# Two more turns between the operands of the head and pooling products and the products, and an embedding unit two products later

## The chip, the cores and the metric

The kernel runs on one core of one Trainium2 chip. The metric is the device time in microseconds (us) of one execution; the median of several runs is compared. Times inside an execution are counted from the start of the profiled span.

## The reference

One decoder layer over 1024 tokens of width 1024, in float32. A normalised input goes through one projection `w_in` to 4608 columns: 512 for a pooling branch, 1024 for a recurrence (RG-LRU), 1024 for its GELU gate and 2048 for two sigmoid gates.

```
pooled_g = (csum - csum shifted by w_g)/count - z_pool_g      4 groups of 128, w = 2, 4, 8, 16
y_pool   = (pooled_g @ pool_w_g) * pool_scale  @ pool_proj
xc       = causal convolution of z_lru, width 4
r, ig    = sigmoid(xc_head @ w_rg + b), sigmoid(xc_head @ w_ig + b)      8 heads of 128
a        = exp(-8 r softplus(-lambda));  b = sqrt(1 - a^2) * ig * xc
y_lru    = scan(a, b) * gelu(z_gelu)  @ lru_proj
h        = x + (gate0 * y_pool + gate1 * y_lru) @ w_out
h        = h + (silu(v @ w_g) * (v @ w_u)) @ w_ffn_out,   v = rms_norm(h)
h        = h + sigmoid(rms_norm(h) @ w_ple_gate) * (p @ w_ple_proj)
out      = rms_norm(h)
```

## The kernel before

**Products.** Channels lie on the 128 partitions, the 1024 tokens along the free axis, in two halves LOW and HIGH of 512. Every float32 product is made of three matmuls on split operands: a factor is cast by ScalarE (`hi`, L115) and the remainder of the cast is taken by VectorE (`lo`, L119). `mm3` (L216) issues hi*hi, hi*lo and lo*hi (L219 to L221); `mm6` (L223, matmuls at L227) does the same for both token halves.

**Units.** TensorE's work is a list of units that `drive()` issues in order. The first projection is done with Strassen's scheme (`strassen`): output tiles go in 18 pairs, each pair needs seven products named by `q` in the order 1, 5, 6, 2, 7, 3, 4, and each product is one unit of 12 matmuls. Pairs go in groups of 3, then six groups of 2, then 3, and a group does its first product for each pair, then the second, and so on: 126 units. Ahead of them stand four units of the per-layer embedding `p @ w_ple_proj` (`ple_unit`, also 12 matmuls each), and four more are set among the first projection's units. Counted from 0 that makes units 0 to 133 up to the end of the first projection. Unit 134 is the first of the pooling branch's projection (`w_pproj`, `mm6`, 24 matmuls each, eight units), and then come the recurrence's projection, `w_out`, the feed-forward layer and the embedding gate.

**The turn of a unit.** In the turn of a unit `drive()` issues, in this order: the inserted units that wait (below), each preceded by the `post` of the unit before it; the `post` of the unit before (it takes results out of PSUM); loads of weights, at most two beyond those that are cast; `second` (`lo`) of weights up to three units ahead and `first` (`hi`) up to four ahead; the unit's `pre`; a slice of background work; the unit's matmuls. Each engine works through its own instructions in the order in which they were issued.

**Background.** Convolution, gates and scan of a head (`chain(c, z)`, eight of them), pooling (`pooling(gi, z)`, four) and the reloads are Python generators in a queue. Only the two at the front are stepped. A turn gives a credit of half a unit's nominal time; a step that yields a number costs that many us; a step that yields `None` means: not again before the next turn. Chains with an odd number first let five turns go by. A head's product is two small units of six matmuls (`half(0)`, `half(1)`), a pooling group's two of three; they are put into `inserted` and go out behind the unit in whose turn they were put in. A chain makes the casts of its weights and LOW tokens in one turn (L688 and L689 are the sigmoids of its product, L706 to L708 tanh, exp and square, L712 and L713 VectorE's steps, L715 the square root, L722 to L726 products and scan), and in the turn that puts in `half(0)` it casts the HIGH tokens.

**The end of the first projection.** When the pooled tiles are spilled and the last group's third product has begun, `begin_mixed` (in the queue behind the last chain that was added before it) lets four reloads follow: each loads one pooled tile (`mx`), and then makes `hi` of both halves (L115) and `lo` of both (L119), over four turns. The first unit of `w_pproj`, unit 134, needs all four, in the order 0 to 3. Its `pre` calls `force`, which steps the two generators at the front until all heads' results `y` are stored and all four `mx` operands are made, before the unit's matmuls are issued:

```
def force(*keys):
    while any(k not in have for k in keys):
        for g in list(background)[:2]:
            step(g)
        while inserted:
            u = inserted.popleft()
            u.emit()
            u.post()
```

```
force(*[("y", c) for c in range(NH)], *[("mx", "op", g) for g in range(NG)])
```

**Shared room.** SBUF tiles of 128x1024 come from one pool of 51 buffers, PSUM has 8 banks, loads go out on SyncE's queue (SP), stores on GpSimd's (POOL).

Of the kernel before, what the change touches and what calls it, by code (L numbers as in the profile page):

```python
# [30 lines left out]
NFIRST = 4  # L31
# [33 lines left out]
def hybrid_block(ctx: ExitStack, tc: tile.TileContext, xT, pT, vec, w_in, w_rgig, w_pool,  # L65
# [10 lines left out]
    def at(name, dt=F32):  # L76
        return ap_.tile([P, T], dt, name=name, tag="a", bufs=NA)

    def ps():
        return pp.tile([P, H], F32, name="ps", tag="ps")  # L80
# [6 lines left out]
    def store(out, x):  # L87
        pool.dma_start(out, x)
# [20 lines left out]
    def col(base, i):  # L109
        return cv[:, base + i:base + i + 1]  # L110
# [3 lines left out]
    def hi(op, x):  # L114
        act.copy(op[:, :x.shape[1]], x)  # L115

    def lo(op, x):
        n = x.shape[1]
        dve.tensor_tensor(op[:, H:H + n], x, op[:, :n].bitcast(F32), ALU.subtract)  # L119
# [95 lines left out]
    def mm3(bank, wop, c, xop, first, last, more=False):  # L215


        a, b = wop[:, c * P:(c + 1) * P], wop[:, H + c * P:H + (c + 1) * P]
        pe.matmul(bank, a, xop[:, :H], start=first, stop=False, skip_group_check=more)  # L219
        pe.matmul(bank, a, xop[:, H:], start=False, stop=False, skip_group_check=more)  # L220
        pe.matmul(bank, b, xop[:, :H], start=False, stop=last, skip_group_check=more)  # L221
# [51 lines left out]
    units = []  # L273
# [377 lines left out]
    def chain(c, z):  # L651
        while "xa" not in have:
            yield None
        if c % 2:
            for _ in range(5):
                yield None
        xc = at("xc")
        act.activation(xc, z, AF.Identity, scale=col(C_CW, 3 * NH + c), bias=col(C_CB, c))
        yield None
        for j in (2, 1, 0):  # L660
            d = 3 - j
            dve.scalar_tensor_tensor(xc[:, d:], z[:, :T - d], col(C_CW, j * NH + c), xc[:, d:],
                                     ALU.mult, ALU.add)
            if j == 2:
                wr = at("wrg")[:, :2 * P]
                nc.sync.dma_start(wr, w_rgig[c])
            yield 1.3
        w = at("wrgo", F32R)
        xo = {0: at("xc0", F32R)}
        hi(w, wr)  # L670
        hi(xo[0], xc[:, LOW])
        yield None
        lo(w, wr)
        lo(xo[0], xc[:, LOW])
        yield 1.1
        r, ig = at("r"), at("ig")

        def half(h):
            banks = []

            def emit():
                banks.extend((ps(), ps()))
                for i in (0, 1):
                    mm3(banks[i], w, i, xo[h], True, True)

            def post():
                s = (LOW, HIGH)[h]
                act.activation(r[:, s], banks[0], AF.Sigmoid, bias=col(C_BR, c))  # L688
                act.activation(ig[:, s], banks[1], AF.Sigmoid, bias=col(C_BI, c))  # L689
                have.add(("rg", c, h))  # L690
            return Unit([], emit, post)

        yield None
        inserted.append(half(0))
        xo[1] = at("xc1", F32R)
        hi(xo[1], xc[:, HIGH])
        yield None
        lo(xo[1], xc[:, HIGH])
        yield 0.7
        yield None  # L700
        inserted.append(half(1))
        while ("rg", c, 1) not in have:
            yield None
        th, q = at("th"), at("q")

        act.activation(th, r, AF.Tanh, scale=psp[:, c:c + 1])  # L706
        act.activation(r, r, AF.Exp, scale=nsp[:, c:c + 1])
        act.activation(q, r, AF.Square)  # L708
        dve.tensor_mul(ig, ig, xc)
        yield 1.2  # L710
        yield None
        dve.scalar_tensor_tensor(th, q, 1.0, th, ALU.add, ALU.mult)  # L712
        dve.tensor_scalar(th, th, 0.0, None, ALU.max)  # L713
        yield 1.9
        act.activation(th, th, AF.Sqrt)  # L715
        pool.memset(th[:, 0:1], 1.0)
        while ("gl", c) not in have:
            yield None
        gl = at("gl")
        nc.sync.dma_start(gl, gl_spill[c])  # L720
        yield None
        dve.tensor_mul(ig, ig, th)  # L722
        yield 1.2
        dve.tensor_tensor_scan(ig, r, ig, 0.0, ALU.mult, ALU.add)
        yield 2.3
        dve.tensor_mul(ig, ig, gl)  # L726
        yield 1.2
        store(y_spill[c], ig)
        have.add(("y", c))
# [4 lines left out]
    def pooling(gi, z):  # L734
        while "xa" not in have:
            yield None
        w = 2 << gi
        cur = z
        for i in range(gi + 1):
            d = 1 << i  # L740
            nxt = at("ws")
            pool.tensor_copy(nxt[:, :d], cur[:, :d])
            dve.tensor_add(nxt[:, d:], cur[:, d:], cur[:, :T - d])
            cur = nxt
            yield 1.3
        wr = at("wrp")[:, :P]
        nc.sync.dma_start(wr, w_pool[:, gi * P:(gi + 1) * P])
        dve.tensor_mul(cur[:, :w], cur[:, :w], icnt[:, :w])
        dve.tensor_sub(cur[:, :w], cur[:, :w], z[:, :w])
        dve.scalar_tensor_tensor(cur[:, w:], cur[:, w:], 1.0 / w, z[:, w:], ALU.mult, ALU.subtract)  # L750
        yield 1.6
        wo = at("wpo", F32R)
        xo = {0: at("pl0", F32R)}
        hi(wo, wr)
        hi(xo[0], cur[:, LOW])
        yield None
        lo(wo, wr)
        lo(xo[0], cur[:, LOW])
        yield 0.9
        mx_ = at("mx")  # L760

        def half(h):
            bank = []

            def emit():
                bank.append(ps())
                mm3(bank[0], wo, 0, xo[h], True, True)

            def post():
                act.activation(mx_[:, (LOW, HIGH)[h]], bank[0], AF.Copy, scale=col(C_PS, gi))  # L770
                if h == 1:
                    store(m_spill[gi], mx_)
                    have.add(("mx", gi))
            return Unit([], emit, post)

        yield None
        inserted.append(half(0))
        xo[1] = at("pl1", F32R)
        hi(xo[1], cur[:, HIGH])
        yield None  # L780
        lo(xo[1], cur[:, HIGH])
        yield 0.7
        yield None
        inserted.append(half(1))
        yield 0.1
# [4 lines left out]
    def then(i):  # L790
        def lru(z):
            background.append(chain(i - ZL, z))
            if i == ZL + NH - 1:
                background.append(begin_mixed())

        def pool_(z):
            background.append(pooling(i, z))

        def gelu(z):
            act.activation(z, z, AF.Gelu_apprx_tanh)  # L800
            store(gl_spill[i - ZG], z)
            have.add(("gl", i - ZG))

        def gate(z):
            act.activation(z, z, AF.Sigmoid, bias=col(C_BG, i - ZS))
            store(g_spill[i - ZS], z)
        return gate if i >= ZS else gelu if i >= ZG else lru if i >= ZL else pool_
# [26 lines left out]

    units[NFIRST].early = early
    for i, u in enumerate(beside):
        units.insert(NFIRST + 1 + 2 * i, u)


    def plain(srcs, nk, xs_of, done, pre=None, side=1, order=None):  # L840
# [434 lines left out]
```

## Time and profile before

| | |
|---|---|
| median of 3 runs | 1410.3 us (1408.74 to 1410.36) |
| profiled execution, its own time | 1409.52 us |
| span of its trace | 1407.8 us |
| TensorE (PE) busy | 1364.6 us, 97% |
| VectorE (DVE) busy | 1032.6 us, 73% |
| ScalarE (ACT) busy | 675.3 us, 48% |
| GpSimd (POOL) busy | 86.5 us, 6% |

The profiled execution's own time is 1.7 us over its span. PE is TensorE's matmuls, PEld its weight loads. A PE record lasts longer (0.39 us) than the distance to the next one, since matmuls are pipelined.

### The profile page before, as it was taken

The page shows a single profiled execution, that of the slowest core. Times are in us where ns is not written, and L with a number is a line of the kernel's source. Part 1 is how long each engine was busy: PE and PEld are TensorE (multiplying, and loading weights), DVE is VectorE, ACT ScalarE, POOL GpSimd, SP SyncE. Part 2 cuts the span into 40 slices and gives each one's busy share as a digit, 9 for nine tenths or more (in the row PEclk, how much of TensorE's full clock was granted, in tenths as well). Part 3 has the DMA queues.
Part 4 walks back from the last instruction along what each step waited for, and adds up shares of the span by engine and source line. Part 5 has one row for each costly group of instructions (what it writes and reads, how often), then busy time and mean ns, then how long its engine had stood idle before and what let it go on. Part 6 is the DMA issues. An engine that isn't in the chain of part 4 may idle for free.

```text
span 1407.8 us, 16468 instructions
## 1 busy us (share of the span) xinstructions
PE 1364.6 (97%) x6006; PEld 1121.5 (80%) x6006; DVE 1032.6 (73%) x1523; ACT 675.3 (48%) x1074; POOL 86.5 (6%) x194
## 2 busy tenths in 40 slices
PE   6999999999999999999999999999999999999986
PEld 4787888888788888888888888888888877887865
DVE  5977788888785544566798888888878767768566
ACT  6558665887867112323554444444454422126331
POOL 0003010010000000000001000010110100000000
PEclk8999999999999999999999999999999999999997
DMA  7122143332549224231134334444577798813203
GB/s 315 75 79 95 61 155 111 115 134 99 200 162 400 89 75 147 105 125 43 60 115 152 132 143 148 150 149 165 194 266 269 295 419 303 326 64 120 72 19 120
DMA packets 64737, 220.55 MB, mean 157 GB/s; under 512 B 7312, under 2 KB 9872, under 8 KB 64656
## 3 DMA queue, kind: packets, MB, share of 16 engines
q1 hardware_dynamic: 45936, 151.80, 30.2%
q0 software_dynamic: 18576, 67.64, 11.9%
q8 instruction: 47, 0.77, 0.2%
q14 instruction: 34, 0.28, 0.1%
q10 hardware_dynamic: 144, 0.06, 0.0%
HBM read 147.65 MB, written 71.83 MB: 156 GB/s over the span
## 4 chain that ended last, share of the span: by engine, by line
PE 85%; DVE 6%; ACT 4%; issue 3%; DMA 1%; POOL 1%; DVEq 0%; SPq 0%; ACTq 0%; POOLq 0%
PE ps L221 22%; PE ps L219 22%; PE ps L220 22%; PE ps L227 17%; DVE w L119 1%; DVE ss L328 1%; DMA lT<-fT 1%; PE ps L367 1%; PE ps L345 1%; DVE pg L1139 0%; ACT pg L1137 0%; DVE h L1140 0%; ACT sq L1145 0%; DVE pg L1136 0%; DMA x<-xT 0%
## 5 line engine op out<-in xcount | busy, mean ns | idle before, releaser
L115 ACT CAST w<-wr 128x512 fp32r<-128x512 f32 (+2 forms) x376 | 221.6, 608 | 339.9 <-DVE wr L194 245.0
L119 DVE TENSOR_TENSOR w<-wr,w 128x512 fp32r<-128x512 f32 (+2 forms) x376 | 249.9, 671 | 44.2 <-ACT w L115 43.4
L221 PE MATMUL ps<-xT,w 128*128 128x512 f32 x640 | 249.5, 390 | 1.5 <-DVE w L119 1.4
L219 PE MATMUL ps<-xT,w 128*128 128x512 f32 x640 | 249.4, 390 | 0.1
L220 PE MATMUL ps<-xT,w 128*128 128x512 f32 x640 | 249.1, 389 | 0.0
L219 PE MATMUL ps<-xB,w 128*128 128x512 f32 x480 | 187.2, 390 | 2.1 <-ACT xB L115 1.2
L220 PE MATMUL ps<-xB,w 128*128 128x512 f32 x480 | 187.4, 391 | 1.9 <-DVE xB L119 1.9
L221 PE MATMUL ps<-xB,w 128*128 128x512 f32 x480 | 187.4, 390 | 0.0
L221 PEld LDWEIGHTS ps<-xT,w 128*128 128x128 f32 x640 | 120.1, 188 | 28.1 <-DVE w L119 3.2
L219 PEld LDWEIGHTS ps<-xT,w 128*128 128x128 f32 x640 | 120.2, 188 | 25.1 <-ACT w L115 0.5
L220 PEld LDWEIGHTS ps<-xT,w 128*128 128x128 f32 x640 | 120.1, 188 | 25.1
L220 PEld LDWEIGHTS ps<-xB,w 128*128 128x128 f32 x480 | 90.3, 188 | 21.8 <-DVE xB L119 3.1
L219 PEld LDWEIGHTS ps<-xB,w 128*128 128x128 f32 x480 | 90.2, 188 | 21.5 <-ACT xB L115 1.6
L221 PEld LDWEIGHTS ps<-xB,w 128*128 128x128 f32 x480 | 90.3, 188 | 19.2 <-DVE w L119 0.6
L227 PE MATMUL ps<-m,w 128*128 128x512 f32 x384 | 87.3, 389 | 0.0
L227 PE MATMUL ps<-y,w 128*128 128x512 f32 x384 | 87.2, 389 | 0.0
L227 PEld LDWEIGHTS ps<-y,w 128*128 128x128 f32 x384 | 72.1, 188 | 15.0
L227 PEld LDWEIGHTS ps<-m,w 128*128 128x128 f32 x384 | 72.0, 188 | 14.9
L1068 DVE TENSOR_TENSOR h<-h,ps 128x512 f32<-128x512 f32 x68 | 46.5, 684 | 42.5 <-PE ps L221 42.4
L194 DVE TENSOR_TENSOR wr<-wr 128x512 f32<-128x512 f32 (+1 forms) x104 | 70.4, 678 | 3.0 <-DMA wr<-w_fout 1.2
L219 PE MATMUL ps<-lT,w 128*128 128x512 f32 x176 | 69.0, 392 | 3.4 <-DMA lT<-fT 2.7
L221 PE MATMUL ps<-lT,w 128*128 128x512 f32 x176 | 68.7, 390 | 0.0
(214 smaller groups left out, 2190.3 us busy)
## 6 DMA issues: line engine op xcount, KB each, us to landing
wr<-w_fin SPq DMA_DIRECT2D x44, 512.0 KB, 5.6
fT<-xT POOLq DMA_DIRECT2D x44, 512.0 KB, 5.0
lT<-fT SPq DMA_DIRECT2D x44, 512.0 KB, 7.9
wr<-w_in SPq DMA_DIRECT2D x36, 512.0 KB, 4.3
fB<-xB POOLq DMA_DIRECT2D x33, 512.0 KB, 5.8
lB<-fB SPq DMA_DIRECT2D x33, 512.0 KB, 6.7
g<-z POOLq DMA_DIRECT2D x16, 512.0 KB, 2.9
g<-g SPq DMA_DIRECT2D x16, 512.0 KB, 6.4
```

Of the source, the lines that this page charges most:

```text
L115: act.copy(op[:, :x.shape[1]], x)
L119: dve.tensor_tensor(op[:, H:H + n], x, op[:, :n].bitcast(F32), ALU.subtract)
L194: f(self.place(out), self.place(a), self.place(b))
L219: pe.matmul(bank, a, xop[:, :H], start=first, stop=False, skip_group_check=more)
L220: pe.matmul(bank, a, xop[:, H:], start=False, stop=False, skip_group_check=more)
L221: pe.matmul(bank, b, xop[:, :H], start=False, stop=last, skip_group_check=more)
L227: pe.matmul(bank, w, xop[:, s], start=f, stop=e)
L328: dve.tensor_add(ss, ss, sq)
L345: pe.matmul(m[:, i:i + 1], self.ss[:, t:t + P], mean, start=True, stop=last is None)
L367: pe.matmul(bank[:, i * P:(i + 1) * P], r[:, b + i:b + i + 1].broadcast_to([P, P]), ident, start=True, stop=True)
L1068: dve.tensor_add(h[t][:, s], h[t][:, s], bank)
```

## The change

`chain` and `pooling` each get two more `yield None`: one before each of the two small products is put in. The operands are made where they were, and each product goes out one unit later than before with respect to them. The four embedding units among the first projection's units stood behind its products 0, 1, 2 and 3; the last of them now stands behind product 5 (behind the second product of all three pairs of the first group, and ahead of their third).

```
@@ chain
         yield None
+        yield None
         inserted.append(half(0))
         xo[1] = at("xc1", F32R)
         hi(xo[1], xc[:, HIGH])
         yield None
         lo(xo[1], xc[:, HIGH])
         yield 0.7
+        yield None
         yield None
         inserted.append(half(1))
@@ pooling
         yield None
+        yield None
         inserted.append(half(0))
         xo[1] = at("pl1", F32R)
         hi(xo[1], cur[:, HIGH])
         yield None
         lo(xo[1], cur[:, HIGH])
         yield 0.7
+        yield None
         yield None
         inserted.append(half(1))
@@
     for i, u in enumerate(beside):
-        units.insert(NFIRST + 1 + 2 * i, u)
+        units.insert(NFIRST + (1, 3, 5, 8)[i] + (i == 3), u)
```

## Rows read from the trace of the kernel before

**Rows 1.** The page, busy time of each engine.

```profile
PE 1364.6 (97%) x6006; PEld 1121.5 (80%) x6006; DVE 1032.6 (73%) x1523; ACT 675.3 (48%) x1074; POOL 86.5 (6%) x194
```

**Rows 2.** Windows of the first projection: busy us of each engine, granted clock, DMA.

```profile
43.00:113.00 70.00, 70.00 (x309) 57.93 (x309) 59.86 (x93) 44.98 (x75) 8.26 (x15) 1.00 0.21 77
113.00:117.00 4.00, 1.95 (x8) 1.08 (x7) 2.97 (x5) 3.71 (x6) 3.36 (x8) 1.00 0.00 0
117.00:360.00 243.00, 242.52 (x1069) 200.12 (x1069) 194.67 (x263) 178.49 (x259) 19.01 (x45) 1.00 0.31 113
360.00:390.00 30.00, 27.50 (x114) 20.49 (x113) 23.49 (x28) 25.42 (x33) 3.14 (x7) 1.00 0.55 210
390.00:429.00 39.00, 39.00 (x174) 32.30 (x173) 28.77 (x42) 28.23 (x42) 1.75 (x4) 1.00 0.59 209
```

**Rows 3.** Waits of PE from 43 to 429 us: total, times, longest.

```profile
PE ps L220 <- DVE xc L119: 1.5, 2, 1.0
PE ps L221 <- DVE w L119: 1.4, 3, 0.7
PE ps L219 <- ACT xc L115: 1.0, 1, 1.0
PE ps L219 <- ACT w L115: 0.9, 1, 0.9
```

**Rows 4.** Timeline of PE at the first head's product: start, duration, instruction, [idle before].

```profile
114.53 0.50 PE L219 MATMUL ps<-xc,wrgo 128*128 128x512 f32 x1 [1.05 <-ACT xc L115]
116.03 0.50 PE L220 MATMUL ps<-xc,wrgo 128*128 128x512 f32 x1 [1.00 <-DVE xc L119]
```

**Rows 5.** Windows: ScalarE from 344 to 381 us.

```profile
344.00:381.00 37.00, 35.17 (x151) 27.55 (x150) 24.72 (x32) 36.27 (x41) 2.55 (x7) 1.00 0.46 171
```

**Rows 6.** Timeline of ScalarE, the late weight cast.

```profile
368.01 1.28 ACT L805 ACT_TABLE_LOAD   x1
369.31 1.15 ACT L805 ACTIVATE z<-z,cv 128x1024 f32<-128x1024 f32 x1
370.36 0.60 ACT L115 CAST w<-wr 128x512 fp32r<-128x512 f32 x1
```

**Rows 7.** Timeline of PE around units 130 and 134.

```profile
409.83 0.39 PE L219 MATMUL ps<-xc,wrgo 128*128 128x512 f32 x1
...
416.63 0.39 PE L219 MATMUL ps<-xc,wrgo 128*128 128x512 f32 x1
...
428.87 6.51 PE L227 MATMUL ps<-mx,w 128*128 128x512 f32 x28
```

**Rows 8.** Timeline of ScalarE, the last chain and the last pooled tile.

```profile
417.55 1.15 ACT L805 ACTIVATE z<-z,cv 128x1024 f32<-128x1024 f32 x1 [0.84 <-DVE z L503]
418.61 0.67 ACT L688 ACTIVATE r<-ps,cv 128x512 f32<-128x512 f32 x1
...
420.26 1.16 ACT L706 ACTIVATE th<-r,sc 128x1024 f32<-128x1024 f32 x1
421.43 1.28 ACT L707 ACT_TABLE_LOAD   x1
422.73 1.15 ACT L707 ACTIVATE r<-r,sc 128x1024 f32<-128x1024 f32 x1
423.91 1.06 ACT L708 ACTIVATE q<-r 128x1024 f32<-128x1024 f32 x1
424.99 1.28 ACT L805 ACT_TABLE_LOAD   x1
...
427.85 1.14 ACT L115 CAST mx<-mx 128x512 fp32r<-128x512 f32 x2
```

**Rows 9.** Timeline of VectorE at the same place.

```profile
425.01 1.23 DVE L712 SCALAR_TENSOR_TENSOR th<-q,th 128x1024 f32<-128x1024 f32 x1 [2.69 <-ACT q L708]
426.27 0.69 DVE L713 TENSOR_SCALAR th<-th 128x1024 f32<-128x1024 f32 x1
...
428.59 1.29 DVE L119 TENSOR_TENSOR mx<-mx 128x512 fp32r<-128x512 f32 x2
```

**Rows 10.** Windows of two places where PE started again after waiting; PEclk is the third number from the right.

```profile
39.00:45.00 6.00, 5.25 (x16) 4.19 (x17) 5.79 (x11) 1.78 (x3) 0.00 (x0) 0.72 0.00 0
1347.00:1356.00 9.00, 8.00 (x23) 6.30 (x24) 6.72 (x11) 3.56 (x7) 0.00 (x0) 0.62 0.00 0
```

**Rows 11.** Timeline of PE, the first matmul of the second of these places.

```profile
1348.00 0.79 PE L221 MATMUL ps<-v,w 128*128 128x512 f32 x1 [3.70 <-DVE w L119]
```

**Rows 12.** Timeline of VectorE, the last remainders of the first group's third operand.

```profile
66.84 1.29 DVE L119 TENSOR_TENSOR xT<-x,xT 128x512 fp32r<-128x512 f32 x2
```

More of the change, by code (lines that the diff above doesn't have):

```diff
@@ L693, in chain @@
         yield None
+        yield None
         inserted.append(half(0))
@@ L699, in chain @@
         yield 0.7
+        yield None
         yield None
@@ L776, in pooling @@
         yield None
+        yield None
         inserted.append(half(0))
@@ L782, in pooling @@
         yield 0.7
+        yield None
         yield None
@@ L836, in hybrid_block @@
     for i, u in enumerate(beside):
-        units.insert(NFIRST + 1 + 2 * i, u)
+        units.insert(NFIRST + (1, 3, 5, 8)[i] + (i == 3), u)
     def plain(srcs, nk, xs_of, done, pre=None, side=1, order=None):
```

## The prediction

> **What bounds the kernel.** The page comes first: TensorE (PE) is busy 97% of the span [rows 1], so only what makes PE wait, or ends a wait of PE, can move the time. All parts of the change lie between 43 and 440 us, so the windows of that stretch come next [rows 2]: PE has no idle time from 43 to 113 us and from 390 to 429, 0.48 us in all from 117 to 360, and two places with idle time, 113 to 117 (4.00 - 1.95 = 2.05 us) and 360 to 390 (2.50 us). One unit is 12 matmuls at 243 us / 1069 = 0.227 us, or 2.72 us; a half of a head's product, six matmuls, is 1.36 us. The waits name the causes [rows 3]: the products of heads wait 2.5 us for casts and remainders of `xc`, and the units at 370 to 386 us wait 2.3 us for casts and remainders of weights. The timeline shows the worst of the first kind [rows 4].
>
> **Part 1: heads and pooling one unit later, at their place.** Waits of 1.05 and 1.00 us stand ahead of the first head's product [rows 4]. The recorded idle time understates it, as a record (0.39 us) outlasts the step to the next (0.227 us): start to start the two gaps and a slow step after them take 2.6 us more than three steps would. The second head's product loses 0.75 us likewise and the third 0.1 us. One unit later (2.72 us) all these operands are ready, and the units that move ahead of the product have had their weights for longer than that. Gain 3.4 us; bounds 2.5 (the recorded waits alone) and 3.4.
>
> **Part 2: ScalarE's crowd at 344 to 381 us.** Here ScalarE is busy 36.27 of 37.00 us [rows 5]. Two chains (5 and 6) run their sigmoid, tanh, exp and square root while gelu and gate tiles come out of the group of units 99 to 112; ten activation tables are loaded, 1.30 us each from start to start, and a weight cast comes behind a gate's sigmoid at 370.36 us, when PE already waits for it [rows 6]. Start to start, units 115 to 119 lose 4.35 us in all (1.46, 1.34, 0.33, 0.59, 0.63).
>
> Where do the chains stand after the change? I stepped through the queue by its rules, turn by turn. For the kernel before, this puts all 24 small products where the trace has them; for example the last chain's, behind units 127 and 129 [rows 7]: from 416.63 us one half (1.36) and four units (10.9) lead to 428.87 us, where unit 134 starts. With the change chains 6 and 5 put in their second halves in turns 114 and 116 (before 106 and 109), so their tanh and exp come after the gelu and gate tiles of turns 110 to 113 instead of among them. Summing ScalarE's work by turn with the spacings of [rows 6, 8], it falls behind PE by about 9 us in turn 117, where it was 13 in turn 113; casts are issued four units ahead (10.9 us), which covers 9 and did not cover 13. What remains is VectorE: a scan stands ahead of one weight's remainder there, about 1 us late. But chain 3 now meets the gelu and gate tiles of turns 82 to 85, at which no chain's exp stood before: the same crowd with one chain, about 0.5 to 1 us late. I take 2.0 us of new waits against the 4.35: gain 2.4 us. Bounds: 4.35 (nothing new waits) and 2 us of loss (both places wait, each for 3).
>
> **Part 3: the end of the first projection.** Each chain now holds one of the two places in the queue for two turns more, and each pooling too. The fourth pooling ends in turn 104 (before 95), chains 6 and 5 in 121 and 125 (before 115 and 118). Only then do the reloads and chain 7 come to the front. Before: reloads start in turns 119, 122, 126 and 129, chain 7's halves go out behind units 127 and 129, and when unit 134 comes only chain 7's last multiply and its store are open. After: the first three reloads start in turns 125, 130 and 133, chain 7's first half goes out behind unit 133, its second isn't put in, and the fourth reload has not begun. So `force` ahead of unit 134 issues all that is left, about twelve rounds of steps: the third tile's `hi` and `lo`, the second half, tanh, exp, square and VectorE's L712 and L713, and only behind those the fourth tile's `hi` (ScalarE) and `lo` (VectorE). Unit 134 needs that tile for the last six of its matmuls' 24.
>
> Let T be the end of unit 133. ScalarE starts about 0.5 us after T, with a copy (0.6) and a gate (1.06 from start to start, 417.55 to 418.61 [rows 8]); the first half's two sigmoids (1.15), a weight cast (0.5) and the third tile's two casts (1.1); the second half's sigmoids (1.15), tanh (1.17), the table load (1.30), exp (1.18) and square (1.07) [rows 8]. That is 10.3, so T + 10.8. VectorE follows with 1.26 and 0.69, then the fourth tile's remainders, 1.29 [rows 9] (its casts run beside the first two): T + 14.1. PE has both halves first (2.72), the first three tiles (4.08) and two matmuls and the bank's turn (0.7), so it wants that remainder at T + 7.5. It waits about 6.6 us. Its DMA is not late: four loads of `mx` stood far ahead of their casts, and ScalarE gets there only at T + 10.8.
>
> A wait this long also costs clock. After PE waited 3.70 us the granted clock was 0.5, that is 1.2 GHz instead of 2.4, for some 6 us [rows 10, 11]: 9 us at a mean of 0.62 are 3.4 us lost, some 0.4 of it while PE still stood. After the several short waits before 40 us the loss was 0.28 x 6 = 1.7 us [rows 10]. PE would stand 4.7 us and then start in pieces. I take 2.5; bounds 1.7 and 3.0.
>
> Sum of part 3: 6.6 + 2.5 = 9.1 us lost. Below, with ScalarE not behind at T, 6.2 + 1.7 = 7.9; above, 7.5 + 3.0, and 1.5 if a buffer for the fourth tile comes free only behind L712: 12. The table load is priced by its row, 1.30 us to the next instruction [rows 8].
> The Trainium skill (ScalarE: Activation LUTs, "What ACT_TABLE_LOAD costs") gives a switch of tables about 1.38 us of drain beside the 1.28 of the load. No drain of that length shows in the row; by the page the one switch in this sequence would cost 1.4 us more and the time be 1415.
>
> Nothing later takes the loss back: after 440 us each stage's PE work waits on PE's own order, all engines shift together, and chain 7's result (some 8 us later) is wanted by the recurrence's projection only 43 us after unit 134 starts.
>
> **Part 4: the last embedding unit.** Two product units come 2.72 us earlier, at a place where PE never waits [rows 2]. The first group's third product, which VectorE feeds to the last moment (its last remainders start at 66.84 us [rows 12], its unit at 67.08), starts when it did, for the same units lie ahead of it. VectorE's order is unchanged, ScalarE's two copies and one store on POOL go out two units later, and POOL's next item comes only at 102 us. Six banks are held by the group and two by the embedding unit, all eight; the next bank is asked for three units on. Zero; if the early weights were short, up to 2.7.
>
> **The sum.** -3.4 - 2.4 + 9.1 = +3.3 us: 1409.5 + 3.3 = 1412.8 for the profiled execution, 1413.6 beside the median, which is 0.8 above it.
>
> **Rivals.**
> *The end is hidden:* the fourth tile is not late, because ScalarE is through with chain 7's activations sooner than summed; then only parts 1 and 2 count, 1410.3 - 5.8 = 1404.5. For it: before, the last `mx` remainders ended at 429.9 us, 3 us ahead of need, and it is one tile in four. Against: its `hi` stands behind a square that cannot run before T + 10, and its price decides: while part 3 costs under 5.8 us the kernel is faster. 0.07.
> *The terms cancel:* the crowd of part 2 goes without a trace (4.35) and part 3 is at its low end: 7.9 - 3.4 - 4.35 = +0.2, 1410.5. With the sizes between that and the forecast's own range, 0.23.
> *The crowds grow:* new waits in both places as long as those of before, 9.1 - 3.4 + 2 = +7.7, 1418. For it: three more chains' phases move, buffers are held longer and loads wait for them. Against: in both places fewer tables are loaded per turn. 0.12.
> *The small products wait as before,* since VectorE and ScalarE order nothing differently: +6.7, 1417. Against: their operands were ready at 116 us, and the first product now comes at 116. 0.03.
>
> **Numbers.** The forecast, 1413.6 with its own range of 1411.5 to 1416, holds 0.55. The bound of 0.2% (2.8 us, about what a measurement of this kernel can tell from no change) lies inside that range, at 1413.1; I put 0.44 of the 0.55 above it, as PE's wait in part 3 is the best founded term and its clock cost can only add. With the third and fourth rival that makes 0.59 for slower; the second rival and the rest of the forecast make 0.34 for no change; the first rival, 0.07, is faster. The range leaves out the first rival and the far end of the third: 1409 to 1418.
>
> **What would show it.** Right: no `xc` wait of PE at 113 to 117 us; no waits for weights of this size at 370 to 386; in the turn of unit 134 a wait of PE of 5 to 7 us for `mx`, named by VectorE's L119 or ScalarE's L115, and PEclk 0.5 behind it. Wrong: unit 134 running 5.4 us without a gap; the wait named by a DMA (then a buffer or the queue decides); waits for weights near 280 us or 390 us of over 2 us; a wait of PE between 56 and 70 us (part 4). The prediction fails if ScalarE has the fourth tile's casts ahead of chain 7's activations, for then nearly all of part 3 is gone.

## The result: slower by 11.3 us

| | before | after |
|---|---|---|
| median of 4 runs each | 1410.33 us | 1421.58 us (1420.24 to 1422.97) |
| ratio, with 95% interval | | 1.0074 (1.0057 to 1.009) |
| profiled execution, its own time | 1409.52 us | 1422.97 us |
| span of its trace | 1407.8 us | 1421.3 us |

The forecast was 1413.6 us with a range of 1409 to 1418. The sign is right; the time lies above the range. The page of the kernel after, busy time of each engine (as [rows 1]):

```profile
PE 1371.1 (96%) x6006; PEld 1126.0 (79%) x6006; DVE 1034.1 (73%) x1523; ACT 673.7 (47%) x1073; POOL 87.2 (6%) x194
```

The work is the same, and PE has a smaller share of a longer span. Windows of the kernel after, from the first head's product to the start of the pooling branch's projection (columns as in [rows 2]):

```profile
113.00:117.00 4.00, 4.00 (x20) 3.29 (x19) 3.27 (x5) 3.71 (x6) 3.34 (x8) 1.00 0.00 0
117.00:280.00 163.00, 163.00 (x721) 134.96 (x720) 126.76 (x172) 114.84 (x168) 13.21 (x31) 1.00 0.31 109
280.00:300.00 20.00, 17.18 (x72) 12.98 (x71) 16.74 (x21) 18.76 (x28) 3.45 (x7) 1.00 0.30 122
300.00:385.00 85.00, 85.00 (x376) 70.38 (x375) 65.12 (x90) 66.23 (x91) 5.40 (x12) 1.00 0.36 128
385.00:412.00 27.00, 23.61 (x96) 18.80 (x95) 21.67 (x27) 15.93 (x25) 1.16 (x3) 0.94 0.55 187
...
429.00:445.00 16.00, 10.34 (x34) 7.05 (x33) 8.70 (x11) 15.88 (x23) 0.92 (x3) 0.84 1.03 420
```

PE's idle time at 113 to 117 us and at 360 to 385 us is gone. In its place PE stands at 280 to 300 us (20.00 - 17.18 = 2.82), at 385 to 412 (3.39) and at 429 to 445 (5.66); in the last two the granted clock falls too. The waits of PE in the same stretch (as [rows 3]; left out are those before 43 us and two of 0.3 us for `xc`):

```profile
PE ps L227 <- ACT mx L115: 4.3, 1, 4.3
PE ps L219 <- DVE z L499: 2.6, 1, 2.6
...
PE ps L221 <- DVE w L119: 1.7, 3, 0.8
...
PE ps L219 <- ACT z L497: 1.1, 1, 1.1
PE ps L227 <- DVE mx L119: 0.8, 1, 0.8
PE ps L219 <- ACT w L115: 0.8, 1, 0.8
```

The 4.3 us for `mx` was forecast. The second row was not: `z` at L499 and L497 are no operands. L497 is ScalarE's copy of product 1 of a pair out of its PSUM bank, L499 VectorE's add of product 2; PE waits there for a bank that has not been read yet.

**Where the time went.** Recorded idle time understates a wait, so the table takes from each trace the distances between the starts of successive matmuls, less the undisturbed step of 0.227 us: waits, plus matmuls at half clock (0.43 us apart). "End" is chain 7's product plus the time from the first `mx` matmul to the first `y` matmul over the 43.52 us that it takes before, less 1.36 us for each half of chain 7 that runs inside it. Columns in us; "sum" is against the kernel before; "time" is the difference of the medians on the same chip.

| kernel | heads 105-210 | 250-300 | 360-412 | end | sum | time |
|---|---|---|---|---|---|---|
| before | 3.5 | 0 | 4.4 | 0 | | |
| after | 0 | 3.9 | 5.5 | 9.5 | +11.0 | +11.3 |
| forecast of after | 0 | 0.5 to 1 | 1 | 9.1 | +3.3 | +3.3 |
| e1_embed | 3.5 | 0 | 4.4 | 0 | 0 | +0.8 |
| e2_heads | 0 | 7.2 | 11.3 | 10.4 | +21.1 | +22.7 |
| e3_pools | 3.4 | 2.0 | 9.5 | 6.8 | +13.7 | +13.3 |
| e4_first | 0 | 1.4 | 5.3 | 0.7 | -0.5 | -0.7 |
| e0_before_end | 3.5 | 0 | 4.4 | 0 | 0 | -0.2 |
| e5_end | 0 | 3.9 | 5.5 | 2.3 | +3.8 | +4.7 |
| e8_before_nogelu | 2.0 | 0 | 3.0 | 0 | -2.9 | -1.1 |
| e7_after_nogelu | 0 | 1.5 | 4.3 | 9.5 | +7.4 | +8.6 |
| e9_scan | 0 | 3.9 | 1.1 | 5.6 | +2.7 | +0.4 |
| e10_conv | 0 | 4.5 | 10.5 | 0 | +7.1 | +6.9 |
| f1_phase3 | 0 | 2.0 | 5.1 | 2.5 | +1.7 | +3.7 |
| e11_kept | 0 | 0 | 4.4 | 0 | -3.5 | -5.3 |
| e12_moved | 0 | 0 | 4.8 | 7.2 | +4.1 | +3.3 |
| f2_phase5 | 0 | 0 | 3.3 | 0 | -4.6 | -2.9 |
| f3_phase5b | 0 | 0 | 1.8 | 1.2 | -4.9 | -3.4 |

For after, the sum agrees with the first `y` matmul, which comes at 483.5 us where it came at 472.4. The profiled execution is 13.45 us longer; of the other 2.4, about 1.6 are a granted clock of 0.94 from 1161 to 1191 us, which the profiled execution of before does not have (1.00 at 1150 to 1180). The difference of the medians, 11.3, is nearer to the sum without it.

The sums lie inside the 95% interval of the time, except for e8, e9 and f1, which miss it by 0.3 to 0.6 us. The table leaves out what lies ahead of 105 us, where the profiled executions differ by 1 us and more though their kernels issue nearly the same. So a difference of under 2 us between two rows is read from the trace and is not shown by the times.

### The profile page after: what moved, and what is told of

Read it like the earlier page. It is cut to its first block, busy times and chain, and to the rows that moved or that the text cites. A ratio compares the mean times of both kernels' runs of the same rounds, so it can differ in the third digit from the quotient of the medians.

```text
span 1421.3 us, 16453 instructions
## 1 busy us (share of the span) xinstructions
PE 1371.1 (96%) x6006; PEld 1126.0 (79%) x6006; DVE 1034.1 (73%) x1523; ACT 673.7 (47%) x1073; POOL 87.2 (6%) x194
## 3 DMA queue, kind: packets, MB, share of 16 engines
q0 software_dynamic: 18576, 67.64, 11.8%
## 4 chain that ended last, share of the span: by engine, by line
PE 78%; DVE 9%; ACT 5%; DMA 4%; issue 3%; POOL 0%; DVEq 0%; SPq 0%; ACTq 0%; POOLq 0%
PE ps L219 20%; PE ps L221 20%; PE ps L220 20%; PE ps L227 17%; DMA lT<-fT 2%; DVE w L119 1%; DVE xc L662 1%; ACT w L115 1%; DMA fB<-xB 1%; DVE ss L328 1%; DMA hr<-h 1%; PE ps L367 1%; PE ps L345 1%; DVE wr L194 1%; DVE pg L1143 1%
```

## The experiments

Each kernel was timed in three rounds against the kernel before on the same chip.

**The change taken apart.** `e1_embed` makes only the third hunk of the change, `e2_heads` only the two lines in `chain`, `e3_pools` only the two in `pooling`, `e4_first` only one extra turn, for one product:

```
@@ e4_first, chain
         yield None
+        if c == 0:
+            yield None
         inserted.append(half(0))
```

> Only the last embedding unit is moved. Theory (three separate causes: new waits at the two crowded places, and the forced work ahead of unit 134): none of them hangs on this unit, so 1410.3 within 1 us, with the waits of before at 113 to 117 and 370 to 386 us. Rival (the moved unit takes the last two PSUM banks, or keeps a buffer, and so starts the later waits): 1413 or more.

> Only the chains of the heads get the two turns. By the queue's rules chain 3's exp falls into turn 82 again (the crowd near 280 us) and the work forced ahead of unit 134 again holds chain 7 and two reloads. Theory: -3.4 for the heads, some 4 near 280 us, 0 to 6 near 390, some 9 at unit 134, less the old 4.35: 1416 to 1421. Rival (the poolings' longer stay is what makes the end late): within 3 us of 1410.

> Only the poolings get the two turns. The waits for xc at 113 to 117 us stay (no gain); chain 3's exp comes in turn 79, before the gelu tiles; when unit 134 comes only the last reload's remainders are open, with chain 7 past its square. Theory: no wait near 280 us, a changed one near 380 us, under 2 us at unit 134: 1408 to 1414. Rival (poolings make the end late): 1417 or more.

> One turn more only ahead of the first head's first product. Theory: its waits go (2.6 us), the end of the projection is as before (one round of forced steps), chains 6 and 5 have exp in turns 107 and 112 and so about the crowd of before: 1407.7, between 1405 and 1410. Rival (any shift of the queue costs what it gains): 1410 or more.

Measured: e1_embed 1411.40, ratio 1.0004 (0.9994 to 1.0013); e2_heads 1433.25, 1.0159 (1.0144 to 1.0174); e3_pools 1423.91, 1.0092 (1.0077 to 1.0107); e4_first 1409.92, 1.000 (0.9991 to 1.001). e2_heads and e3_pools came out far above what was expected (1416 to 1421 and 1408 to 1414), and for e3_pools the rival held: the poolings alone make the end late, by 6.8 us. e4_first stands at the upper edge of its range, as near to its rival.

The embedding unit costs nothing that can be told from zero. The chains' lines alone cost twice what the whole change costs, and the poolings' lines alone more than the whole. So the cost is no sum over the edits: each edit moves the chains against the units, and what counts is where they meet. The timelines of PE from 360 to 412 us show it. First e2_heads, then e3_pools, the two longest waits of each:

```profile
399.26 0.50 PE L219 MATMUL ps<-xB,w 128*128 128x512 f32 x1 [1.66 <-ACT w L115]
...
407.95 0.77 PE L219 MATMUL ps<-xB,w 128*128 128x512 f32 x1 [5.41 <-DVE z L499]
```

```profile
396.75 0.50 PE L221 MATMUL ps<-xB,w 128*128 128x512 f32 x1 [2.21 <-DVE w L119]
...
404.21 0.47 PE L219 MATMUL ps<-xB,w 128*128 128x512 f32 x1 [2.16 <-DVE z L499]
```

In both, the add of L499 ends one of them. Near 280 us the whole 7.2 of e2_heads is one wait for a bank, whose copy L497 is late, with half clock behind it:

```profile
291.64 0.79 PE L219 MATMUL ps<-xT,w 128*128 128x512 f32 x1 [3.81 <-ACT z L497]
```

e4_first shows the same in small: it gains the 3.5 us at the heads, and new waits (1.4 at 250 to 300 us, 0.9 more at 360 to 412, 0.7 at the end) take 3.0 of them back.

**The end.** `e5_end` is after, except that unit 134 finishes only the reloads of `mx`, chain 7 goes on in the background, and from there three generators are stepped instead of two. A reload of `y` now waits until its `y` is stored, which `force` had seen to before (not among the lines below). `e0_before_end` puts the same treatment into before.

```
@@ begin_mixed (the generators are kept in mx_left)
-            background.append(reload(m_spill[gi], mixed, gi, "mx"))
+            mx_left.append(reload(m_spill[gi], mixed, gi, "mx"))
+            background.append(mx_left[-1])
@@ pre_pproj
-            force(*[("y", c) for c in range(NH)], *[("mx", "op", g) for g in range(NG)])
+            for g in mx_left:
+                if g in background:
+                    background.remove(g)
+                    finish(g)
+            width[0] = 3
```

> The changed kernel, but ahead of unit 134 only the four mx reloads are carried to their end; chain 7 goes on in the background among the units of the pooling projection (three generators are stepped per turn there). Theory (unit 134 waits for the fourth tile's casts behind chain 7's activations, 9.5 us with the clock): the forced casts then stand right behind the gate tiles, unit 134 waits 0 to 2 us and the clock stays: 1421.6 - 8 = 1413.5, between 1411.5 and 1416. Rival (the late loads of the tiles, or the buffers, set that wait): 1419 or more.

> The kernel before with the same treatment of the end, as a control. Its unit 134 doesn't wait: 1410.3, within 1.5 us either way, if the chain that goes on later delays nothing.

Measured: e5_end 1415.16, ratio 1.0032 (1.0018 to 1.0045), 6.4 us under after; e0_before_end 1410.22, 1.000 (0.9991 to 1.001). The window and PE's timeline of e5_end at that place:

```profile
429.00:445.00 16.00, 14.50 (x62) 11.23 (x61) 7.18 (x12) 10.19 (x18) 1.06 (x2) 1.00 1.03 420
```

```profile
430.30 2.88 PE L227 MATMUL ps<-mx,w 128*128 128x512 f32 x12
434.59 10.69 PE L227 MATMUL ps<-mx,w 128*128 128x512 f32 x43 [1.41 <-ACT mx L115]
```

With chain 7's activations out of the way one wait of 1.41 us is left (2.3 us in the table), and the clock stays at 1.00 where after has 0.84. The waits at 280 and 390 us are those of after (3.9 and 5.5). So the end and the rest are separate costs, and chain 7's sequence ahead of the fourth tile is the cause of most of the end.

**ScalarE's load.** `e7_after_nogelu` and `e8_before_nogelu` are after and before with the GELU replaced by a copy, so GELU's values and its table loads are left out:

```
-            act.activation(z, z, AF.Gelu_apprx_tanh)
+            act.copy(z, z)
```

> The changed kernel with GELU replaced by a plain copy, which leaves the GELU out, so that ScalarE loads two tables less at each of the crowded places where gelu tiles come out. Theory (near 280 us and 390 us ScalarE's lag holds back the copies out of PSUM and the weight casts): the waits of PE near 280 us (3.9) go altogether, those near 390 us (5.5) fall below 3, the loss at unit 134 stays 9 to 10: 1412 to 1415. Rival (chain lengths and buffers, not ScalarE's lag): 1419 or more.

> The kernel before with GELU replaced by a plain copy (left out), the control: the waits of 4.4 us at 370 to 386 us go or fall below 1.5, those of the heads (3.5) stay: 1406 to 1408.

Measured: e7 1419.01, ratio 1.0059 (1.0044 to 1.0074); e8 1409.30, 0.9992 (0.9983 to 1.0001). Near 280 us the loss falls from 3.9 to 1.5, at 360 to 412 only from 5.5 to 4.3: there the wait for L499 stays at 2.51 us. So GELU with its tables makes most of the loss at the first place and little at the second. Both expectations were missed: e7 was to take 1412 to 1415 and came out at its rival's 1419, and e8 was to take 1406 to 1408, with under 1.5 us left at 370 to 386 us (3.0 are left).

**The bank near 390 us.** In the timeline of after, PE first and then VectorE:

```profile
395.84 0.39 PE L221 MATMUL ps<-xB,w 128*128 128x512 f32 x1
398.83 0.75 PE L219 MATMUL ps<-xB,w 128*128 128x512 f32 x1 [2.60 <-DVE z L499]
399.38 0.63 PE L220 MATMUL ps<-xB,w 128*128 128x512 f32 x1
...
402.32 0.39 PE L221 MATMUL ps<-xB,w 128*128 128x512 f32 x1
```

```profile
393.81 0.68 DVE L119 TENSOR_TENSOR w<-wr,w 128x512 fp32r<-128x512 f32 x1
394.55 1.23 DVE L724 TENSOR_TENSOR ig<-ig,th 128x1024 f32<-128x1024 f32 x1
395.81 2.29 DVE L726 TENSOR_TENSOR_SCAN ig<-r,ig 128x1024 f32<-128x1024 f32 x1
398.02 0.66 DVE L499 TENSOR_TENSOR z<-z,ps 128x512 f32<-128x512 f32 x1
```

VectorE does chain 5's product and scan (1.23 + 2.29 us) and only then the add that frees a bank. In the last group, of three pairs, the third product 2 finds all eight banks taken until the first one's is added; PE resumes 0.81 us after that add starts. `e9_scan` is e5_end with that product and scan one turn later:

```
@@ chain, ahead of L724
+        if c == 5:
+            yield None
         dve.tensor_mul(ig, ig, th)
```

> The kernel with the end mended (e5), and chain 5's product with its square root and its scan held one turn longer, so that VectorE adds unit 122's bank into z ahead of them. Theory (unit 124, the third of three products that each take a fresh bank, gets none before that add, and the add stands behind a scan that waits for a square root): the wait of 2.6 us for L501 and the half clock behind it (1.4) go, 1415.2 - 3.8 = 1411.4, between 1410 and 1413. Rival (ScalarE's lag alone decides near 390 us): the wait stays or moves, 1414 or more.

Measured: 1412.27, ratio 1.0007 (0.9998 to 1.0017). VectorE in e9_scan (lines are 2 to 4 higher; L728 and L730 are the product and scan, L501 the add):

```profile
394.32 0.68 DVE L501 TENSOR_TENSOR z<-z,ps 128x512 f32<-128x512 f32 x1
...
395.91 1.22 DVE L728 TENSOR_TENSOR ig<-ig,th 128x1024 f32<-128x1024 f32 x1
397.17 2.29 DVE L730 TENSOR_TENSOR_SCAN ig<-r,ig 128x1024 f32<-128x1024 f32 x1
```

The add now stands ahead of the scan; the wait for it and the half clock are gone, and 360 to 412 falls from 5.5 to 1.1. That settles this place. The 1.1 left is a weight's remainder behind an earlier scan:

```profile
388.12 0.50 PE L221 MATMUL ps<-xT,w 128*128 128x512 f32 x1 [0.81 <-DVE w L119]
```

But unit 134 waits 2.99 us for `mx` where e5_end waited 1.41, and the end takes 3.3 of the 4.4 us back: the casts of the last two tiles start 5.2 us after unit 134's first matmul (429.73 against 424.53), where in e5_end it was 3.6. Against before, e9_scan is 4.3 us faster than e5_end in time and 1.1 in the sum. In the profiled executions 1.5 us more lie ahead of 105 us, where the two kernels issue the same; the rest is open.

**Near 280 us.** ScalarE of after stands idle there for 2.20 us, behind an add that VectorE issues after three steps of chain 4's convolution, and then has the tables of chain 3 among those of gelu and gate:

```profile
268.54 1.06 ACT L804 ACTIVATE z<-z 128x1024 f32<-128x1024 f32 x1 [2.20 <-DVE z L503]
...
283.86 0.60 ACT L115 CAST w<-wr 128x512 fp32r<-128x512 f32 x1
...
287.93 1.28 ACT L717 ACT_TABLE_LOAD   x1
289.23 1.06 ACT L717 ACTIVATE th<-th 128x1024 f32<-128x1024 f32 x1
290.19 0.57 ACT L497 COPY z<-ps 128x512 f32<-128x512 f32 x1
```

```profile
284.51 0.50 PE L219 MATMUL ps<-xT,w 128*128 128x512 f32 x1 [0.76 <-ACT w L115]
...
285.78 0.50 PE L221 MATMUL ps<-xT,w 128*128 128x512 f32 x1 [0.54 <-DVE w L119]
...
290.81 0.50 PE L219 MATMUL ps<-xT,w 128*128 128x512 f32 x1 [1.13 <-ACT z L497]
...
294.66 0.50 PE L221 MATMUL ps<-xT,w 128*128 128x512 f32 x1 [0.39 <-DVE w L119]
```

PE (second view) loses 2.5 us to weights and 1.4 to a bank whose copy, L497, stands behind a table load and a square root. Two kernels try the two halves of this, both on top of e5_end: `e10_conv` spreads chain 4's convolution over three turns, `f1_phase3` lets chain 3 start without its five idle turns.

```
@@ e10_conv, chain, in the loop over j
+            if c == 4 and j:
+                yield None
@@ f1_phase3, chain
-            for _ in range(5):
+            for _ in range({3: 0}.get(c, 5)):
```

> The kernel with the end mended (e5), and chain 4's three convolution steps in three turns instead of one, so that the add which completes the first gelu tile near 268 us stands behind one of them and not three. Theory (ScalarE stands 2.2 us for that add, and its lag is what holds back copies and casts): the waits of PE near 280 us fall from 3.9 to 1 to 2 us. Later turns shift, so the time itself says little: 1410 to 1416. Rival (the number of table loads alone): 3.5 us or more stay.

> The kernel with the end mended (e5), with chain 3 started without its five idle turns, so that its exp comes in turn 79 and its square root in turn 80, ahead of the gelu and gate tiles of turns 82 to 85. Theory (the meeting of one chain's activations with these tiles makes the wait): PE waits near 280 us fall from 3.9 to under 0.7 us. Near 390 us chains 6 and 5 have exp in turns 114 and 115, so waits of 2 to 6 us stay there: 1409 to 1414. Rival (chain lengths, held buffers or banks): 2.5 us or more near 280.

Measured: e10_conv 1418.80, ratio 1.0049 (1.0034 to 1.0064); f1_phase3 1414.78, 1.0026 (1.0016 to 1.0036). In e10_conv ScalarE's idle time falls from 2.20 to 0.49 us and the waits for weights at 284 to 286 us are gone, but PE then waits once, longer, for the same kind of copy (line 2 higher), and about 1.7 us of half clock follow:

```profile
289.19 0.50 PE L219 MATMUL ps<-xT,w 128*128 128x512 f32 x1 [2.66 <-ACT z L499]
```

The time lies above what was expected (1410 to 1416), and the 4.5 us near 280 are the rival's (3.5 or more stay). But that kernel moved chain 4 as well, also at 360 to 412 us (10.5), so it doesn't isolate the idle time. f1_phase3 halves the loss near 280 us, 3.9 to 2.0: chain 3's meeting with the gelu and gate tiles makes about half of it (under 0.7 was expected, 2.5 or more by the rival). What makes the other half is not settled.

**What is worth keeping.** If the cost lies in moved phases, the heads' gain should stand alone when the queue afterwards is left as it was. `e11_kept` is before with the turn added only where a product waited, and given back by the second chain's start:

```
@@ chain
-            for _ in range(5):
+            for _ in range({1: 4, 5: 5}.get(c, 5)):
@@
         yield None
+        if c == 0:
+            yield None
         inserted.append(half(0))
@@
+        if c == 1:
+            yield None
         yield None
         inserted.append(half(1))
```

> The kernel before with one turn more only at the first head's first product and the second head's second one, and one turn less in the second chain's start, so that from turn 51 on everything is issued as before. Theory (the waits of the two heads are worth 3.5 us by themselves, and every later loss comes from the later turns): the waits for xc go, those at 370 to 386 us stay, no others: 1406.9, between 1405.5 and 1408.5. Rival (the gain is taken back by waits of weights even so): 1409.5 or more.

Measured: 1406.57, ratio 0.9966 (0.9955 to 0.9977): faster than both kernels, as expected. The gain of 5.3 us in time is more than the 3.5 that were removed, but its interval (3.2 to 6.4) holds them. Its windows at the heads and at the second place:

```profile
113.00:117.00 4.00, 4.00 (x19) 3.29 (x18) 3.28 (x5) 3.70 (x6) 3.35 (x8) 1.00 0.00 0
117.00:360.00 243.00, 243.00 (x1073) 201.20 (x1072) 195.16 (x264) 182.40 (x264) 19.84 (x47) 1.00 0.33 115
360.00:390.00 30.00, 27.50 (x114) 20.46 (x113) 25.48 (x31) 25.49 (x36) 2.76 (x6) 1.00 0.58 214
390.00:425.00 35.00, 35.00 (x156) 29.00 (x155) 25.73 (x38) 24.29 (x35) 1.60 (x3) 1.00 0.62 207
```

The heads' idle time is gone, that at 360 to 390 us (2.50) is as in [rows 2], and nothing new waits. Three more kernels build on it and move chain 5 to take that wait away too: `e12_moved` by five turns, with e5_end's end and three generators from the reloads on; `f2_phase5` by two and `f3_phase5b` by three turns, with three generators from the last part of the first projection to the recurrence's projection.

> As e11_kept, with the end mended, three generators stepped from the start of the reloads on, and chain 5 started five turns later, so that its exp comes in turn 117, behind the gelu and gate tiles and ahead of the last group's fresh banks. Theory: the waits at 370 to 386 us go too (4.4), and unit 134 waits under 1 us: 1403, between 1401 and 1406. Rival (chain 5 meets another crowd there): 1407 or more.

> As e11_kept, with chain 5 started two turns later (exp in turn 113, square root 116, scan 117: behind the gelu tiles and ahead of the fresh banks of units 122 to 124), and three generators stepped per turn from turn 119 up to the recurrence's projection, so that the reloads (122 to 128) don't wait for it. Theory: the waits at 366 to 382 us fall from 4.4 to 0 to 2 us and unit 134 doesn't wait: 1402.5 to 1405. Rival (it meets another crowd): 1406.6 or more.

> As f2_phase5 with one turn more (exp in turn 116, square root 117, scan 118; the last reload in turn 133). Theory: 1402.5 to 1406, up to 2 us more than f2 for a late last reload at unit 134. Rival: 1407 or more.

Measured: e12_moved 1415.17, ratio 1.003 (1.0017 to 1.0043); f2_phase5 1408.20, 0.9976 (0.9965 to 0.9986); f3_phase5b 1407.69, 0.9976 (0.9964 to 0.9987). All three expectations were missed, and each time lies in the range of its rival. e12_moved lost 7.2 us at the end (unit 134 waits 4.83 us for a remainder of `mx`); f2_phase5 lost 1.53 us of idle time to a weight and 1.27 to a bank. In f3_phase5b a wait of 1.57 us ahead of 394.24 is put down to a cast of `xc`, which that unit doesn't read; VectorE's add L500 starts 0.83 us before PE resumes there (0.81 in after), so a bank is the likelier cause. None beats e11_kept.

The waits for this bank fall on one and the same matmul: the first of the third product 2 in the last group. It waits in after (2.60 us), e5_end (2.59), e2_heads (5.41), e3_pools (2.16), e4_first (1.14), e7_after_nogelu (2.51), e10_conv (2.80), f1_phase3 (1.67), e12_moved (2.15), f2_phase5 (1.27) and f3_phase5b (1.57), and not in before, e11_kept and e9_scan.

## Why the prediction was too low

**Part 1, the heads: right.** 3.4 us forecast, 3.5 found ([rows 4] against the window 113 to 117 us of after); the first head's product starts at 116.29 us without a wait.

**Part 2, the crowds: the step that failed.** The old waits at 370 to 386 us did go, as forecast. The failed step is "I take 2.0 us of new waits against the 4.35". The new waits came where the step said, at the tiles of turns 82 to 85 (near 280 us) and at the scan (near 390), but they measure 3.9 and 5.5 us, 9.4 in all. Instead of a gain of 2.4 there is a loss of about 5. The step failed in what it took for cover. It set the lag of ScalarE and VectorE only against weights, which are cast four units (10.9 us) ahead. The reads that free a PSUM bank have no such lead: PE comes back for a bank one to three units after its product, and the copies and adds (L497, L499) stand in the same in-order queues behind table loads, square roots and scans. At 390 us that is 4.4 of the 5.5 us (2.6 of recorded wait and about 1.7 of half clock), which e9_scan took away by moving the scan behind the add; the other 1.1 is the late remainder of a weight that the step had, at about 1 us. Near 280 us, where 0.5 to 1 us was taken, the bank makes 1.4 us; the other 2.5 are weights, so the lag was also larger there than summed, and e7 and f1 put the loss down in part to GELU's tables and chain 3's meeting them. What makes the rest of it stays open. The upper rival (both places as bad as before, 1418) had the places and the sign, but it spoke of held buffers and late loads and not of banks, and its price, a loss of 2 us, was too small. Of the signs of being wrong one came, and only as a sum: waits for weights near 280 us of over 2 us (2.5, start to start, in three waits). The wait of a bank stood among none of them.

**Part 3, the end: right.** 9.1 us forecast, 9.5 found. With T, the end of unit 133, at 427.74 us, the order on ScalarE is the one that was written down. PE, ScalarE and VectorE of after:

```profile
431.62 4.25 PE L227 MATMUL ps<-mx,w 128*128 128x512 f32 x18
440.17 1.32 PE L227 MATMUL ps<-mx,w 128*128 128x512 f32 x2 [4.30 <-ACT mx L115]
442.25 1.40 PE L227 MATMUL ps<-mx,w 128*128 128x512 f32 x2 [0.76 <-DVE mx L119]
```

```profile
434.90 1.16 ACT L708 ACTIVATE th<-r,sc 128x1024 f32<-128x1024 f32 x1
436.08 1.28 ACT L709 ACT_TABLE_LOAD   x1
437.37 1.15 ACT L709 ACTIVATE r<-r,sc 128x1024 f32<-128x1024 f32 x1
...
439.51 1.12 ACT L115 CAST mx<-mx 128x512 fp32r<-128x512 f32 x2
```

```profile
440.90 0.69 DVE L715 TENSOR_SCALAR th<-th 128x1024 f32<-128x1024 f32 x1
441.51 1.29 DVE L119 TENSOR_TENSOR mx<-mx 128x512 fp32r<-128x512 f32 x2
```

PE runs the 18 matmuls of three tiles, then waits for the fourth's casts (T + 11.8, forecast 10.8) and remainders (T + 15.1, forecast 14.1). Start to start, at 0.227 us a matmul, the two waits take 4.5 and 1.6 us; with 1.1 at chain 7's second half that is 7.2 where 6.6 was forecast, and 2.3 are clock where 2.5 was. ScalarE and VectorE were each 1 us later than summed; PE came 1.1 us later too, so these two misses cancel. The table load takes 1.29 us to the next instruction, as in [rows 8]. The Trainium skill (ScalarE: Activation LUTs, "What ACT_TABLE_LOAD costs") adds 1.38 us of drain to a load of 1.28; this row again shows none, so the row's price was the one to use.

**Part 4, the embedding unit: right.** Zero forecast; e1_embed is level, and after has no wait from 56 to 70 us.

The sum by measured terms is -3.5 + 3.9 + (5.5 - 4.4) + 9.5 = 11.0.

## What to carry to other kernels

Ask of each kind of instruction behind a lagging engine how far ahead of its reader it is issued: here weight casts had four units of lead, reads that free a PSUM bank one to three, and the smaller lead made the larger of the new losses (5.8 of 9.4 us). Moving a step in an in-order queue by whole turns moves every later meeting of phases, so price the new meetings, not only the wait that is removed. Delay only the product that waits and give the turn back, so that what follows stays where it was.

## What was not expected of the hardware

The length of a wait alone did not tell whether half clock (0.43 us from matmul to matmul) followed. In e3_pools a wait of 2.21 us at 396.75 left the steps at 0.227 us, and one of 2.16 us at 404.21 was followed by seven slow ones. Waits of 1.13 us (after, 290.81), 1.66 us (e2_heads, 399.26) and 1.67 us (f1_phase3, 398.56) left full speed, but one of 1.67 us (e10_conv, 394.17) was followed by slow steps from the fifth matmul on; after 2.60 us (after, 398.83) and 2.66 us (e10_conv, 289.19) they came too, and cost about 1.7 us each. The start of the drop varies too: behind the 3.70 us wait of [rows 11] the very next matmul was slow, and behind the same wait in after (3.72 us, at 1360.64) the drop came some three matmuls later, with a mean clock of 0.81 over 9 us where [rows 10] has 0.62.
